# Bias rows from float32r parts over 128 rows, and vectors and filter turned in full blocks

## The chip, the cores and the metric

The kernel runs on one core of a Trainium2 chip. The metric is the device time of one execution in microseconds (us); 1726.06 us is the median of three runs of the kernel before. The core's engines are PE (TensorE, matrix products and transposes into PSUM), DVE (VectorE), ACT (ScalarE), POOL (GpSimd) and SP (which issues most transfers); each works through its own queue in order, and they wait for each other by semaphores. Transfers issued by POOL go through a queue of their own (q0 in the profile).

## The reference

One layer of a hybrid decoder trunk, with S = D = 1024, 8 heads and a convolution of width 31. Cut to what the change touches:

```python
h = rms_norm(x, attn_norm_w)
q, k, v, u, g = jnp.split(h @ w_in, splits, axis=-1)
...
rel = q_pos[:, None] - k_pos[None, :]
bias = jnp.transpose(bias_tab[t5_bucket(rel)], (2, 0, 1))      # bias_tab: rel_bias, 32 x 8
s = jnp.einsum('bhqd,bhkd->bhqk', qb, kf) * scale + bias
s = jnp.where(rel >= 0, s, -jnp.inf)                           # softmax, values, subln follow
...
c = causal_depthwise_conv(u_a * sigmoid(u_b), conv_w, conv_b)  # conv_w: 31 x 1024
c = silu(layer_norm(c, conv_ln_w, conv_ln_b))
y_b = c @ w_proj_conv
...
x = x + (sigmoid(g_a + b_a) * y_a + sigmoid(g_b + b_b) * y_b) @ w_out
x = x + (silu(gate) * up) @ w_down                             # gate, up from rms_norm(x)
```

The bias of a head depends on the distance of query and key alone, so it is one row of values for each head, laid out along the diagonals. Each bias row entry is `rel_bias` at the bucket of its distance, and a large negative number where the key lies ahead of the query. Inputs and outputs are float32.

## The kernel before

The program is one long stream of tiles of 128 partitions, written for each engine through a scheduler that sorts the instructions of each engine by a model of their times; `after(ins)` ties the instructions of a block behind an earlier one of their engine. Matrix products are made from float32r parts: an operand is split into a high part (ACT copies it to float32r, L120) and a low part (the difference, by DVE at L125 or by POOL at L131), and three products (high-high, high-low, low-high) are summed in PSUM (`mm3`, L167 to L170).

Order of the work around the change:

- `opening` (from L1084) loads and normalises the eight token tiles of x, turns them with full 128x128 transposes (`turn_x`, L724) and makes the first value columns (`v_tile`, L1110). After the third tile it calls `load_vectors` (from L229): POOL clears `rows` (64x128) and loads into it the small vectors, 128 numbers to a row (conv bias, layer-norm weight and bias, gate bias, subln, q and k norm), and into `cwrow` (31x1024) the convolution filter, a tap to a row. `vectors_last` is the last POOL instruction of that.
- At the end of `opening`, `vectors` (L256) turns them: one transpose of the 64 rows (L259), copied to `pvec`, where a vector is a column and so a scalar for each partition; and eight transposes of 31x128 (L267), copied to `cw`. Then the buffers of the opening are given back, and the pools `tt` and `st` are opened in their place.
- `first_stage` goes on with the remaining value columns (`v_item`, V1 and V2) and, for c = 1 to 7, `u_pair` (from L996): the convolution's input channels by a scheme of seven half-size products (L984) in place of eight. Their operands are sums and differences that POOL makes (L900 to L926 once, L965 to L968 for each pair) and splits (L131). A `u_pair` uses the half tiles `p1`, `u2` and `u3` of the pool `st`; `u2` has one buffer, the other two have two. ACT copies a product to `u2` at L1010 and to `u3` at L1013, and POOL multiplies them at L1021.
- Beside that, DVE runs the convolution, 31 taps a channel tile (`conv_taps`, L588 on ACT for the first, L594 on DVE for the others). The first four tiles are summed in PSUM, and ACT copies each to a tile `done` (L598), which has the single buffer of the tag `acc` in the pool `cv`; DMA stores it (L600).
- The loop over `first_stage` calls `bias_rows` at its steps 18, 19 and 20, each for 384 of the 1152 columns. `buckets` is an input of 33x1152 that holds one 1 in each column (the bucket of that distance, or row 32 where the key lies ahead). At the first call POOL fills `rb` (33x8) and loads `rel_bias` (L765, L766), and DVE changes its sign (L767). Each call then loads 384 columns of `buckets` into a half tile `u3` (L769), makes the product of `rb` and these in full float32, which runs as two matmul records (L771), copies the 8x384 result to a half tile `u2` (ACT, L772), and stores it to `b_d` (POOL, L773). Later `bias_skew` (L776) spreads each head's row over 128 rows of `t_d`, and `load_bias` reads it skewed, before the attention of that head.

The stages after that (attention beside the query, key and gate columns, the projections, the feed-forward part) are not touched.

Of the kernel before, what the change touches and what calls it, by code (L numbers as in the profile page):

```python
# [10 lines left out]
F32 = mybir.dt.float32  # L11
F32R = mybir.dt.float32r
AF = mybir.ActivationFunctionType
ALU = mybir.AluOpType
AX = mybir.AxisListType

P = 128
S = 1024
D = 1024
H = 8  # L20
HD = 64
VD = 128
CW = 31
FF = 2816
NFF = FF // P
NB = 32
EPS = 1e-6
LAM_INIT = 0.8 - 0.6 * math.exp(-0.3 * 0)
BIG = 1.0e30
# [28 lines left out]
def kernel(  # L58
# [57 lines left out]
    def f32(ap):  # L116
        return ap.bitcast(F32)

    def split_hi(dst, src):
        act.copy(dst, src)  # L120
# [3 lines left out]
    def split_lo(dst, src, hi):  # L124
        last_lo[0] = dve.tensor_tensor(dst, src, f32(hi), op=ALU.subtract).ins  # L125
# [9 lines left out]
    def after(ins):  # L135

        return nullcontext() if ins is None else tc.issue_after(ins)

    def last_of(engine):
        for ins in reversed(nc.cur_bb.bb.instructions):  # L140
            if ins.engine == engine:
                return ins
# [70 lines left out]
        act.copy(wb[:, 512 * g : 512 * (g + 1)], pt[:])  # L213

    NROW = 64
    rows = ap.tile([NROW, P], F32, name="rows", bufs=1)
    col = {}
    at = [0]

# [3 lines left out]
        col[key] = r0  # L223
        at[0] += n

    cwrow = ap.tile([CW, D], F32, name="cwrow", bufs=1)
    lamt = ap.tile([P, 4, HD], F32, name="lamt", bufs=1)

    def load_vectors():  # L229
        pool.memset(rows[:], 0.0)  # L230
        pool.dma_start(cwrow[:], conv_w[0])
        vec_rows("conv_b", conv_b, 8)
        vec_rows("ln_w", conv_ln_w, 8)
        vec_rows("ln_b", conv_ln_b, 8)
        vec_rows("gate_b", gate_b, 16)
        vec_rows("subln", subln_w, 1)
        for key, src in (("qn", q_norm_w), ("kn", k_norm_w)):
            r0 = at[0]
            for j in range(2):
                pool.dma_start(rows[r0 : r0 + 1, j * HD : (j + 1) * HD], src)  # L240
            col[key] = r0
            at[0] += 1
        for j, src in enumerate((lam_q1, lam_k1, lam_q2, lam_k2)):
            pool.dma_start(lamt[:, j, :], src.to_broadcast([P, HD]))
# [11 lines left out]
    def vectors():  # L256

        pt = pm()
        pe.transpose(pt[:, :NROW], rows[:], ident[:NROW, :NROW])  # L259
        dve.tensor_copy(pvec[:], pt[:, :NROW])  # L260
        dve.tensor_scalar(pcol("subln"), pcol("subln"), 1.0 - LAM_INIT, None, op0=ALU.mult)
        dve.tensor_scalar(pcol("kn"), pcol("kn"), -(HD ** -0.5), None, op0=ALU.mult)
        c_ = col["ln_w"]
        dve.tensor_scalar(pvec[:, c_ : c_ + 8], pvec[:, c_ : c_ + 8], -0.125, None, op0=ALU.mult)
        pt = pm()
        for k in range(NKT):
            pe.transpose(pt[:, k * 32 : k * 32 + CW], cwrow[:, k * P : (k + 1) * P], ident[:CW, :CW])  # L267
        dve.tensor_copy(
            cw[:, :, :CW], pt[:, : NKT * 32].rearrange("p (k t) -> p k t", t=32)[:, :, :CW]
        )  # L270
        for j in range(2):
            dve.tensor_tensor(lprod[:, j, :], lamt[:, 2 * j, :], lamt[:, 2 * j + 1, :], op=ALU.mult)
        dve.tensor_reduce(lsum[:], lprod[:], axis=AX.X, op=ALU.add)
# [461 lines left out]
    def tiles_from(pool_, names):  # L735
        return lambda: [pool_.tile([P, 512], F32R, tag=t_, name=nm(t_), bufs=2) for t_ in names]
# [14 lines left out]
    def v_item(j):  # L751
        halves = [ws.next(), ws.next()]
        for i2 in range(NT // 2):
# [3 lines left out]
            v_split(o, j, i2)  # L757
            yield

    rb = sm.tile([NB + 1, H], F32, tag="rb", name="rb", bufs=1)  # L760

    def bias_rows(c0):

        if c0 == 0:
            pool.memset(rb[:], -BIG)  # L765
            pool.dma_start(rb[:NB, :], rel_bias)  # L766
            dve.tensor_scalar(rb[:], rb[:], -1.0, None, op0=ALU.mult)  # L767
        oh, gr = half("u3")[: NB + 1, :384], half("u2")[:H, :384]
        pool.dma_start(oh, buckets[:, c0 : c0 + 384])  # L769
        o = pm()  # L770
        pe.matmul(o[:H, :384], rb[:], oh, start=True, stop=True)  # L771
        act.copy(gr, o[:H, :384])  # L772
        pool.dma_start(b_d[:, c0 : c0 + 384], gr)  # L773

    def bias_skew(h):
        pool.dma_start(t_d[h][:], b_d[h : h + 1, :].to_broadcast([P, TL]))  # L776
# [103 lines left out]
    def half(tag):  # L880
        return f32(st[0].tile([P, 512], F32R, tag=tag, name=nm(tag), bufs=1 if tag == "u2" else 2)[:])
# [202 lines left out]
    def opening():  # L1084
# [69 lines left out]
        )  # L1154
        with after(last_of(mybir.EngineType.Pool)):
            load_vectors()
        vectors_last = last_of(mybir.EngineType.Pool)
        xload(4)
        steps(
# [67 lines left out]
        tt.append(tt_ctx.enter_context(tc.tile_pool(name="tt", bufs=1, reuse_waits="tile")))  # L1227
        st.append(st_ctx.enter_context(tc.tile_pool(name="st", bufs=1, side="right", reuse_waits="tile")))
        v_tiles[0] = tiles_from(st[0], ("p1", "u3"))
        low_by_pool[0] = True  # L1230
        ws.ahead = 0
        yield from u_half(0, uw, 1)
# [5 lines left out]
    for _ in first_stage():  # L1238
        n += 1
        if n in (18, 19, 20):  # L1240
            with after(bias_anchor[0]):
                bias_rows(384 * (n - 18))
        if n >= 23 and n % 3 == 2 and (n - 23) // 3 < 2:
            with after(last_of(mybir.EngineType.Pool)):
                bias_skew((n - 23) // 3)
        due += 3.25
        with after(last_of(mybir.EngineType.DVE)):
            bg.step(int(due))
        due -= int(due)
# [889 lines left out]
```

## Time and profile before

| what | value |
|---|---|
| median of three runs | 1726.06 us (1725.62 to 1727.33) |
| the profiled execution's own time | 1724.98 us |
| its span in the trace | 1723.2 us |
| PE, share of the span busy | 99% |
| DVE, ACT, POOL | 74%, 51%, 13% |
| bias products (L771) | 6 records of 484 ns on average, 130.3 to 146.6 us |
| turn of the small vectors (L259, L267) | 9 transposes, 53.2 to 53.8 us |

The page gives, for each group of instructions, a line of the kernel, the engine, the operation, what is written from what, the shape of the operands (for matmuls also rows x columns of the weights), the count, and after the bar the time busy, the mean duration and the idle time ahead of it with what ended it. A timeline row has the start, the duration, the engine, line and operation, and in brackets the idle time before it and what released it. The half tiles appear there by the first letters of their tags (`u<-pm` is the copy of a bias row to `u2`).

### The profile page before, as it was taken

The page shows a single profiled execution, that of the slowest core. Times are in us where ns is not written, and L with a number is a line of the kernel's source. Part 1 is how long each engine was busy: PE and PEld are TensorE (multiplying, and loading weights), DVE is VectorE, ACT ScalarE, POOL GpSimd, SP SyncE. Part 2 cuts the span into 40 slices and gives each one's busy share as a digit, 9 for nine tenths or more (in the row PEclk, how much of TensorE's full clock was granted, in tenths as well). Part 3 has the DMA queues.
Part 4 walks back from the last instruction along what each step waited for, and adds up shares of the span by engine and source line. Part 5 has one row for each costly group of instructions (what it writes and reads, how often), then busy time and mean ns, then how long its engine had stood idle before and what let it go on. Part 6 is the DMA issues. An engine that isn't in the chain of part 4 may idle for free.

```text
span 1723.2 us, 25849 instructions
## 1 busy us (share of the span) xinstructions
PE 1713.9 (99%) x9243; PEld 1478.2 (86%) x9243; DVE 1276.2 (74%) x2128; ACT 873.2 (51%) x1958; POOL 219.2 (13%) x207
## 2 busy tenths in 40 slices
PE   9999999999999999999999999999999999999999
PEld 7997889998998998988788888888888888888887
DVE  7675889898988987977677769966666666575544
ACT  6333335767877886865556325633333333333332
POOL 4997851000000000000000000000000000000000
PEclk9999999999999999999999999999999999999999
DMA  6344445436345345354863683244455445597663
GB/s 209 117 128 134 131 151 143 113 103 174 107 128 147 116 125 148 99 146 145 316 225 128 196 301 108 77 141 156 149 174 167 153 143 165 175 371 271 216 217 128
DMA packets 261603, 281.64 MB, mean 163 GB/s; under 512 B 16545, under 2 KB 181985, under 8 KB 261474
## 3 DMA queue, kind: packets, MB, share of 16 engines
q1 hardware_dynamic: 254160, 267.71, 48.4%
q0 software_dynamic: 5680, 9.39, 2.6%
q10 hardware_dynamic: 1634, 2.89, 0.5%
q8 instruction: 73, 1.20, 0.3%
q14 instruction: 56, 0.46, 0.1%
HBM read 181.84 MB, written 85.50 MB: 155 GB/s over the span
## 4 chain that ended last, share of the span: by engine, by line
PE 93%; DVE 2%; DMA 2%; ACT 1%; issue 1%; SPq 0%; DVEq 0%; ACTq 0%
PE acc L984 30%; PE acc L488 12%; PE pg L168 12%; PE pg L170 12%; PE pg L169 12%; PE wo L1854 3%; PE sc L1294 2%; PE sc L1293 2%; PE pT L1332 2%; DVE acc L594 1%; PE pg L1110 1%; PE pW L168 1%; PE pW L170 1%; PE pW L169 1%; PE pQ L819 1%; DMA room<-in_w_out_dram 1%
## 5 line engine op out<-in xcount | busy, mean ns | idle before, releaser
L594 DVE SCALAR_TENSOR_TENSOR acc<-u,cw,acc 128x1023 f32<-128x1023 f32 (+14 forms) x240 | 303.5, 1264 | 23.0 <-ACT acc L588 20.4
L168 PE MATMUL pg<-whi,hT_hi 128*128 128x256 f32 x704 | 199.2, 284 | 0.8 <-DVE v L125 0.8
L169 PE MATMUL pg<-wlo,hT_hi 128*128 128x256 f32 x704 | 199.9, 284 | 0.0
L170 PE MATMUL pg<-whi,hT_lo 128*128 128x256 f32 x704 | 199.9, 284 | 0.0
L125 DVE TENSOR_TENSOR wlo<-draw,whi 128x1024 fp32r<-128x1024 f32 x75 | 91.8, 1224 | 86.0 <-ACT whi L120 78.6
L120 ACT CAST whi<-draw 128x1024 fp32r<-128x1024 f32 x75 | 79.1, 1055 | 129.5 <-PE acc L488 121.0
L168 PEld LDWEIGHTS pg<-whi,hT_hi 128*128 128x128 f32 x704 | 133.8, 191 | 2.6 <-DVE v L125 1.0
L169 PEld LDWEIGHTS pg<-wlo,hT_hi 128*128 128x128 f32 x704 | 134.2, 191 | 1.7
L170 PEld LDWEIGHTS pg<-whi,hT_lo 128*128 128x128 f32 x704 | 134.3, 191 | 1.5
L120 ACT CAST whi<-wraw 128x1024 fp32r<-128x1024 f32 x90 | 94.7, 1053 | 71.1 <-PE pg L169 37.0
L488 PE MATMUL acc<-wlo,whi 128*128 128x512 f32 x308 | 119.8, 389 | 0.0
L488 PE MATMUL acc<-whi,wlo 128*128 128x512 f32 x308 | 119.8, 389 | 0.0
L168 PE MATMUL pg<-hT_hi,whi 128*128 128x512 f32 x288 | 114.5, 398 | 0.0
L170 PE MATMUL pg<-hT_hi,wlo 128*128 128x512 f32 x288 | 113.9, 395 | 0.0
L169 PE MATMUL pg<-hT_lo,whi 128*128 128x512 f32 x288 | 113.9, 395 | 0.0
L1300 ACT ACTIVATE E<-E,mn 128x640 f32<-128x640 f32 (+7 forms) x128 | 99.5, 777 | 26.0 <-DVE mn L1295 25.6
L120 ACT CAST whi<-s 128x1024 fp32r<-128x1024 f32 x54 | 56.8, 1053 | 105.1 <-PE acc L984 102.0
L125 DVE TENSOR_TENSOR wlo<-wraw,whi 128x1024 fp32r<-128x1024 f32 x75 | 93.3, 1246 | 14.4 <-ACT whi L120 14.2
L984 PE MATMUL acc<-h_hi,whi 128*128 128x512 f32 x240 | 93.4, 389 | 0.0
L984 PE MATMUL acc<-h_lo,whi 128*128 128x512 f32 x240 | 93.4, 389 | 0.0
L1295 DVE CUSTOM_DVE_ANT_0 E<-sc,tb 128x512 f32<-128x512 f32 (+3 forms) x128 | 74.2, 585 | 23.6 <-PE pT L1332 13.8
L984 PE MATMUL acc<-h_hi,wlo 128*128 128x512 f32 x240 | 90.1, 389 | 0.0
(370 smaller groups left out, 4591.6 us busy)
## 6 DMA issues: line engine op xcount, KB each, us to landing
wraw<-in_w_gate_up_dram SPq DMA_DIRECT2D x44, 512.0 KB, 4.6
wraw<-in_w_in_dram SPq DMA_DIRECT2D x38, 512.0 KB, 4.1
qs<-qs SPq DMA_DIRECT2D x96, 128.0 KB, 2.3
wd<-in_w_down_dram SPq DMA_DIRECT2D x44, 256.0 KB, 3.1
tdT<-wd SPq DMA_DIRECT2D x88, 128.0 KB, 4.4
draw<-sdS SPq DMA_DIRECT2D x44, 256.0 KB, 3.8
draw<-tdT SPq DMA_DIRECT2D x44, 256.0 KB, 3.5
wraw<-in_w_in_dram SPq DMA_DIRECT2D x32, 256.0 KB, 3.2
```

The lines of the kernel that those rows point to most:

```text
L120: act.copy(dst, src)
L125: last_lo[0] = dve.tensor_tensor(dst, src, f32(hi), op=ALU.subtract).ins
L168: pe.matmul(o, lh, rh, start=start, stop=False)
L169: pe.matmul(o, lh, rl, start=False, stop=False)
L170: last_mm[0] = pe.matmul(o, ll, rh, start=False, stop=stop).ins
L488: m = pe.matmul(o[s_][i][:], l_[:, ts], r_[:, 512:], start=start and j + y_ == 0, stop=j == n - 1 and y_ == 2, skip_group_check=not start,)
L594: dve.scalar_tensor_tensor(a_, us[c][:, : S - n], cw[:, c, t : t + 1], a_, op0=ALU.mult, op1=ALU.add)
L984: last_mm[0] = pe.matmul(o[:], a_[x_][:, k, :], b_[y_][:, k, :], start=start and k + x_ + y_ == 0, stop=k == 3 and x_ == 1, skip_group_che ...
L1293: pe.matmul(o[:, :w], qh[:, qs], k, start=True, stop=False)
L1295: dve.tensor_tensor_reduce(e[:, ks], o[:, :w], tb[:, S - nk + c0 : S - nk + c0 + w], 1.0, mn[:, j : j + 1] if c0 else 3.0e38, ALU.add, ALU ...
L1300: act.activation(e[:, :nk], e[:, :nk], AF.Exp, bias=mn[:, j : j + 1], scale=-1.0, accum_out=l[:, j : j + 1])
L1854: last_mm[0] = pe.matmul(o[s_][i][:], A[u_], B[v_], start=start and j + y_ == 0, stop=j == 3 and y_ == 2, skip_group_check=not start,).ins
```

## The change

Three parts.

1. `rows` becomes 128x128, and its turn (L259) a full 128x128 transpose. `cwrow` becomes 128x2x128: the filter is loaded in four transfers, which put four blocks of 128 channels under each other, 32 partitions apart, and the eight transposes of 31 rows (L267) become two full ones. POOL clears `cwrow` first.
2. `bias_rows` makes each product as two float32r products, of a high and a low part of `rb` in 72 columns (8 of them used, the others zero), over all 128 rows (33 used, the others zero). The columns are cut as 512, 512 and 128 in place of three times 384. Only the first 8 rows of the result are copied.
3. The operands are made ahead: `bias_ones` loads the first 1024 columns of `buckets` into a cleared 128x1024 tile `oh`, right after `load_vectors`, in the buffer of the tag `acc`; `bias_tiles` clears and fills the two parts of `rb` and the last 128 columns of `buckets` (`tail`) when the pool `st` is opened. The load of `rel_bias` moves behind `load_vectors`, and `bias_rows` loads nothing.

```diff
-    rows = ap.tile([NROW, P], F32, name="rows", bufs=1)
+    rows = ap.tile([P, P], F32, name="rows", bufs=1)
...
-    cwrow = ap.tile([CW, D], F32, name="cwrow", bufs=1)
+    cwrow = ap.tile([P, 2, P], F32, name="cwrow", bufs=1)
...
         pool.memset(rows[:], 0.0)
-        pool.dma_start(cwrow[:], conv_w[0])
+        pool.memset(cwrow[:], 0.0)
+        for q in range(4):
+            pool.dma_start(
+                cwrow[32 * q : 32 * q + CW, :, :],
+                conv_w[0].rearrange("t (j q c) -> t q j c", q=4, c=P)[:, q],
+            )
...
-        pe.transpose(pt[:, :NROW], rows[:], ident[:NROW, :NROW])
+        pe.transpose(pt[:, :P], rows[:], ident[:])
...
-        for k in range(NKT):
-            pe.transpose(pt[:, k * 32 : k * 32 + CW], cwrow[:, k * P : (k + 1) * P], ident[:CW, :CW])
+        for j in range(2):
+            pe.transpose(pt[:, j * P : (j + 1) * P], cwrow[:, j, :], ident[:])
...
+    rb2 = []
+    MB = 72
+
+    def bias_ones():
+        oh = cv.tile([P, S], F32R, tag="acc", name="oh", bufs=1)
+        pool.memset(f32(oh[:]), 0.0)
+        pool.dma_start(oh[: NB + 1, :], buckets[:, :S])
+        rb2.append(oh)
+
+    def bias_tiles():
+        parts = st[0].tile([P, 2, MB], F32R, tag="rb2", name="rb2", bufs=1)
+        tail = st[0].tile([P, TL - S], F32R, tag="oht", name="oht", bufs=1)
+        for t_ in (parts, tail):
+            dve.memset(f32(t_[:]), 0.0)
+        pool.dma_start(tail[: NB + 1, :], buckets[:, S:])
+        with after(last_of(mybir.EngineType.DVE)):
+            dve.tensor_scalar(rb[:], rb[:], -1.0, None, op0=ALU.mult)
+        hi, lo = [parts[: NB + 1, z, :H] for z in range(2)]
+        split_hi(hi, rb[:])
+        split_lo(lo, rb[:], hi)
+        rb2.extend((parts, tail))
...
     def bias_rows(c0):
 
-        if c0 == 0:
-            pool.memset(rb[:], -BIG)
-            pool.dma_start(rb[:NB, :], rel_bias)
-            dve.tensor_scalar(rb[:], rb[:], -1.0, None, op0=ALU.mult)
-        oh, gr = half("u3")[: NB + 1, :384], half("u2")[:H, :384]
-        pool.dma_start(oh, buckets[:, c0 : c0 + 384])
+        cs, n = slice(c0, min(c0 + 512, TL)), min(512, TL - c0)
+        gr = half("u2")[:H, :n]
         o = pm()
-        pe.matmul(o[:H, :384], rb[:], oh, start=True, stop=True)
-        act.copy(gr, o[:H, :384])
-        pool.dma_start(b_d[:, c0 : c0 + 384], gr)
+        for z in range(2):
+            pe.matmul(o[:MB, :n], rb2[1][:, z, :], rb2[0][:, cs] if n == 512 else rb2[2][:], start=z == 0, stop=z == 1)
+        act.copy(gr, o[:H, :n])
+        pool.dma_start(b_d[:, cs], gr)
...
         with after(last_of(mybir.EngineType.Pool)):
             load_vectors()
+            pool.memset(rb[:], -BIG)
+            pool.dma_start(rb[:NB, :], rel_bias)
+            bias_ones()
         vectors_last = last_of(mybir.EngineType.Pool)
...
+        bias_tiles()
         low_by_pool[0] = True
...
-                bias_rows(384 * (n - 18))
+                bias_rows(512 * (n - 18))
```

## The prediction

> **What bounds the kernel now.** I read the head of the page first, then the busy times by stretch, then PE's timeline at the two places that the change touches, and last the other engines' rows beside them. The head of the page:
>
> ```profile
> span 1723.2 us, 25849 instructions
> ...
> PE 1713.9 (99%) x9243; PEld 1478.2 (86%) x9243; DVE 1276.2 (74%) x2128; ACT 873.2 (51%) x1958; POOL 219.2 (13%) x207
> ```
>
> PE (TensorE's matmuls) is busy 99% of the span; nothing else is near. Where PE's 9.3 us of idle time lie, the busy times by stretch tell, here for 60 to 1240 us (the columns: from:to, its length, then PE, PEld, DVE, ACT and POOL busy with their counts, granted clock, DMA share, GB/s):
>
> ```profile
> 60.00:150.00 90.00, 90.00 (x572) 79.92 (x571) 55.91 (x51) 34.70 (x45) 82.26 (x47) 1.00 0.44 140
> 150.00:300.00 150.00, 149.14 (x860) 131.93 (x859) 128.37 (x130) 64.93 (x138) 82.58 (x53) 1.00 0.47 137
> 300.00:820.00 520.00, 519.59 (x3472) 475.95 (x3471) 445.60 (x982) 377.88 (x1213) 19.45 (x73) 1.00 0.46 130
> 820.00:1000.00 180.00, 178.87 (x800) 146.74 (x799) 128.88 (x215) 91.36 (x146) 0.58 (x1) 1.00 0.63 209
> 1000.00:1240.00 240.00, 239.36 (x1087) 197.98 (x1086) 182.18 (x287) 104.07 (x165) 0.00 (x0) 1.00 0.48 160
> ```
>
> The stretch 60 to 150 us holds no idle time of PE at all, and both places of the change lie in or just before it. From 150 to 1240 us PE idles 0.86 + 0.41 + 1.13 + 0.64 = 3.04 us. The granted clock is 1.00 in each. So the price of an edit is the time that it adds to or takes from PE's queue, and every other edit counts only if it makes PE wait. A matmul's own duration misleads here, since matmuls overlap: what one costs is the distance between starts.
>
> **The turn of the small vectors.** PE's timeline around it:
>
> ```profile
> 51.16 1.12 PE L1110 MATMUL pg<-vwl,hT_hi 128*128 128x256 f32 x8
> 52.12 1.12 PE L1110 MATMUL pg<-vwh,hT_lo 128*128 128x256 f32 x8
> 53.17 0.27 PE L259 MATMUL pm<-ident,rows 64*128 64x64 f32 x1
> 53.37 0.67 PE L267 MATMUL pm<-ident,cwrow 31*128 31x31 f32 x8
> 53.97 0.50 PE L168 MATMUL pg<-hT_hi,whi 128*128 128x512 f32 x1
> 54.31 0.40 PE L169 MATMUL pg<-hT_lo,whi 128*128 128x512 f32 x1
> ```
>
> Eight 256-column products take 52.12 - 51.16 = 0.96 us, 0.12 each, so the place of the last ends at 53.08. L259 starts 0.09 later. It takes 0.20, the eight L267 take 0.60, and the first L168 after them holds PE for 0.34, where a 512-column product otherwise holds it 0.23 (below): 0.11 more. Together 1.00 us. After the change three full transposes stand there. Such a thing is in the trace:
>
> ```profile
> 41.27 1.04 PE L724 MATMUL px<-ident,xt 128*128 128x128 f32 x8
> 42.06 0.73 PE L1110 MATMUL pg<-vwl,hT_hi 128*128 128x256 f32 x4
> 42.62 1.11 PE L1110 MATMUL pg<-vwh,hT_lo 128*128 128x256 f32 x8
> ```
>
> Eight full transposes take 0.79 us (0.10 each), and the four products after them 0.56 where 4 x 0.12 = 0.48 would do: leaving the transposes costs 0.08. Three: 0.30 + 0.08 = 0.38 us. The term is 0.38 - 1.00 = **-0.62 us**.
>
> **The bias rows.** Three times, of which the first and the last are:
>
> ```profile
> 129.73 0.39 PE L984 MATMUL acc<-hT_lo,whi 128*128 128x512 f32 x1
> 129.96 0.39 PE L984 MATMUL acc<-hT_hi,wlo 128*128 128x512 f32 x1
> 130.28 0.81 PE L771 MATMUL pm<-u,rb 33*8 33x384 f32 x2
> 131.02 0.50 PE L984 MATMUL acc<-T4h,sh 128*128 128x512 f32 x1
> 131.35 0.39 PE L984 MATMUL acc<-T4l,sh 128*128 128x512 f32 x1
> ...
> 146.29 0.81 PE L771 MATMUL pm<-u,rb 33*8 33x384 f32 x2
> 147.03 0.50 PE L984 MATMUL acc<-hT_hi,wlo 128*128 128x512 f32 x1
> ```
>
> A 512-column product of two float32r operands holds PE for 129.96 - 129.73 = 0.23 us. One full-float32 product (two records, 33 rows) holds it for 0.74, the product before it for 0.32 (0.09 more) and the one after it for 0.33 (0.10 more): 0.93 us. The last one holds it for the same 0.74, so I count 3 x 0.93 = 2.79 us. Afterwards there are two pairs of 512 columns, 4 x 0.23 = 0.92, and one pair of 128 columns. That width in float32r stands in the attention stage:
>
> ```profile
> 372.43 0.22 PE L1293 MATMUL sc<-ks,qs 128*128 128x128 f32 x1
> 372.49 0.27 PE L1294 MATMUL sc<-ks,qs 128*128 128x128 f32 x1
> 372.60 0.45 PE L1293 MATMUL sc<-ks,qs 128*128 128x512 f32 x1
> ```
>
> They hold PE 0.06 and 0.11; a pair is 0.12 to 0.22, I take 0.17. No row shows weights of 128x72. Their bounds are nothing extra, as between any two full float32r products, and the 0.19 of the rows above for each of three groups (0.57). I take nothing, since both operands now fill all rows and have the neighbours' type. Sum 1.09, and the term is 1.09 - 2.79 = **-1.70 us** (-1.13 with the upper bound).
>
> The Trainium skill speaks against the filled rows: "TensorE: Matmul & The Clock Gate", section "Why this matters for your kernels", has a single matmul over 32 rows take the same time as one over 128, and "TensorEngine Tiling (Array Packing)", section "Key Properties", has a change of tiling mode drain the array. By the first, filling the rows gives nothing and the sum below would be that of rival 1; by the second, the 0.09 and 0.10 go and the sum stands. The trace bears out the second only in part: the full transposes, with no change of rows, also cost 0.08 on leaving.
>
> **What lies beside PE.** Rows of the timelines of POOL, DVE and ACT, those between them left out. First POOL ahead of its first sum:
>
> ```profile
> 13.12 0.72 POOL L231 DMA_DIRECT2D cwrow<-in_conv_w_dram  x1
> 15.98 0.13 POOL L765 MEMSET rb<- 33x8 f32 x1
> 22.95 0.51 POOL L766 DMA_DIRECT2D rb<-in_rel_bias_dram x1
> 36.78 0.19 POOL L1184 COPY seen<-xt 128x1 f32<-128x1 f32 x1 [13.32 <-DVE xt L714]
> ```
>
> The load of `rb` was issued at 22.95 already, so that move is nothing. New on POOL before 36.78 are three more issues of the filter (3 x 0.72 = 2.16), a 256-column and a 1024-column memset, and one bucket issue. A memset is bounded by 0.13 (8 columns) below and a whole sum over 1024 columns on POOL, 2.41 (below), above. Together 2.16 + 0.51 + two memsets are 2.9 to 7.5 us in 13.32 of idle time: nothing, and no loss either as long as it ends before 36.78. The filter's bytes stay the same, in shorter pieces, and are needed only at 53.4. Then DVE after the turn, and POOL at the last bias row:
>
> ```profile
> 60.61 1.99 DVE L125 TENSOR_TENSOR wlo<-wraw,whi 128x1024 fp32r<-128x1024 f32 x1 [1.37 <-ACT whi L120]
> 147.35 2.41 POOL L131 TENSOR_TENSOR wlo<-s,whi 128x1024 fp32r<-128x1024 f32 x1 [1.83 <-ACT whi L120]
> 149.72 0.54 POOL L773 DMA_DIRECT2D b_d<-u  x1
> ```
>
> DVE gets two memsets, the sign change (moved) and two small splits, ACT one small cast: each between POOL's 0.13 above and 0.28, the share of 144 columns in the 1.99 of 1024 (an estimate from that row), so about 1 us on DVE between 54 and 60 us. It idled 1.37 us ahead of 60.61: nothing, and at most that 1 us if the idle time were gone. POOL loses three bucket issues at 120 to 140 us and gets one for `tail`, which waits for a DVE memset with POOL's sums queued behind it, and for those ACT and PE; later POOL idles 1.83 us ahead of such a sum, so a stall there under that is hidden, and a longer one costs its excess.
>
> `oh` takes the one buffer of the tag `acc`, so ACT's copy L598 of the first convolution tile now waits for the second bias product:
>
> ```profile
> 125.15 1.02 ACT L598 COPY done<-acc 128x1024 f32<-128x1024 f32 x1 [0.46 <-DVE acc L594]
> 136.70 0.81 PE L771 MATMUL pm<-u,rb 33*8 33x384 f32 x2
> 140.41 1.21 ACT L588 ACTIVATE acc<-u,pvec,cw 128x1024 f32<-128x1024 f32 x1 [2.28 <-DMA u<-u_d]
> 151.49 0.59 ACT L1010 COPY u<-acc 128x512 f32<-128x512 f32 x1 [3.17 <-DMA b_d<-u]
> 154.88 0.39 PE L984 MATMUL acc<-T3h,whi 128*128 128x512 f32 x1
> ```
>
> The copy moves from 125.15 to about 137.4 and is done by 138.5, before L588, which waits for a transfer until 140.41: 1.9 us of cover, and nothing for PE.
>
> **Sum.** -0.62 - 1.70 = -2.32 us on PE. The profiled execution took 1724.98 us (span 1723.2 and 1.78 around it), the median of three runs is 1726.06; the sum moves either by the same. That execution would take 1722.66; it stands 1.08 under the median, so the forecast, made as a median, is 1726.06 - 2.32 = **1723.7 us**, 0.13% less. A measurement of this kernel can tell about 0.2%, 3.45 us, from no change.
>
> **The rivals.** (1) Filling the rows does not remove the 0.19 at each group: the bias term is -1.13, the sum -1.75, the time 1724.3. For it: the 0.08 after full transposes. Against it: the neighbours' type is the same now. The small-row rule of the Trainium skill's "TensorE: Matmul & The Clock Gate", told above, leads to this time.
>
> (2) The gain is given back in the chain through the single buffer `u2`: product, ACT's copy, POOL's store, landing, three times, and only then L1010, after which PE may go on in that bank at 154.88. For it: L1010 waited 3.17 us for the store, and the last store stands behind a sum of 2.41 us on POOL. The cover is 154.88 - 152.08 = 2.8 us, and PE now comes up to 1.7 us sooner: 1.1 is left. If the chain grows by 1.1 to 6.9 us, PE waits for up to 5.8 and the time lies between 1723.7 and 1729.5: I price it at 1726, below the middle, since three such delays are less likely than one. Against it: POOL is rid of three issues, and the third copy is of 128 columns.
>
> (3) The same chain, on the other side: if each of three stores falls behind one more such sum, 3 x 2.41 = 7.2 us, and the wait of 1.83 us for ACT comes with one of them, it grows by 9.0 us, PE loses 7.9, and the time is 1723.7 + 7.9 = **1731.6 us**. It is slower than before by over 0.2% from 6.9 us of growth.
>
> (4) Later waits close up: PE's 3.04 us of gaps from 150 to 1240 us come from other engines' order, which a new order may improve. All of them gone gives 1720.7; over 1.1 us of them is needed for 0.2%. For it: that order hangs on many waits. Against it: nothing in the change aims there, and gaps may grow as well.
>
> **How the numbers follow.** Forecast 0.47 (1722.9 to 1724.5), (1) 0.12, (2) 0.17, (3) 0.08, (4) 0.16. Faster by over 0.2% is (4), 0.16; slower is (3), 0.08; the rest, 0.76, is within. The range takes the forecast, (1), most of (2) and more than half of (4): 1721.4 to 1727.6.
>
> **What would show it.** The turn at 53 us should hold PE 0.4 us instead of 1.0, with no gap ahead of it. Each bias pair should hold it 0.46 (0.17 the narrow one), with neighbours at 0.23; a neighbour at 0.32 shows (1). PE's idle time between 60 and 150 us should stay at nothing, and L1010 should wait no longer than 3.2 us; PE idle after a bias row shows (2) or (3). The forecast is wrong if PE's idle time from 150 to 1240 us differs from 3.04 by more than 1 us.

## The result, and the profile after

The changed kernel takes 1740.77 us (median of five runs, 1740.29 to 1742.70) against 1726.06, a ratio of 1.0089 (95% interval 1.0078 to 1.0100): slower by 0.9%, where 1723.7 us had been forecast, a difference that a measurement can't tell from none. Four single executions on record, one each of the kernel before, turn_only, tail_sp and best2, took 3687 to 6091 us, and the ratios below leave them out. The head of the page after, with the PE row of the costliest groups that tells most:

```profile
span 1740.9 us, 25841 instructions
...
PE 1713.0 (98%) x9237; PEld 1479.3 (85%) x9237; DVE 1296.2 (74%) x2131; ACT 873.0 (50%) x1959; POOL 223.2 (13%) x211
...
L169 PE MATMUL pg<-wlo,hT_hi 128*128 128x256 f32 x704 | 201.0, 286 | 15.7 <-DVE wlo L125 15.7
```

PE is busy for as long as before (1713.0 against 1713.9 us), so the 17.7 us by which its span is longer are idle time: 1740.9 - 1713.0 = 27.9 us against 9.3. (The execution profiled is the slowest of the five, 1742.70 us; the medians differ by 14.7.) The last number of the L169 row says where: 15.7 us in a single wait, for DVE's split of a weight block (`wlo`, L125). The busy times by stretch, first the stretch that had no gap before, then the same cut at the gap (same columns as in the prediction):

```profile
60.00:150.00 90.00, 74.31 (x501) 69.54 (x500) 66.77 (x46) 27.22 (x35) 67.39 (x35) 0.91 0.33 103
```

```profile
66.30:82.20 15.90, 0.28 (x3) 0.07 (x1) 15.90 (x3) 0.30 (x1) 14.75 (x7) 0.60 0.00 1
82.20:86.50 4.30, 4.24 (x20) 4.24 (x21) 0.61 (x2) 0.00 (x0) 0.00 (x0) 0.50 0.56 183
86.50:100.00 13.50, 13.50 (x114) 13.50 (x114) 8.73 (x9) 6.10 (x7) 7.16 (x3) 1.00 0.49 157
```

From 66.3 to 82.2 us PE does nothing, and only DVE and POOL are "busy". Then, for 4.3 us, PE works at a granted clock of 0.50: twenty matmuls where a full clock does some 36 (0.12 us each). DVE's timeline there, and then POOL's:

```profile
59.99 2.06 DVE L781 TENSOR_SCALAR rb<-rb 33x8 f32<-33x8 f32 x1
62.36 18.72 DVE L125 TENSOR_TENSOR rb<-rb,rb 33x8 fp32r<-33x8 f32 x1 [0.31 <-ACT rb L120]
81.00 1.21 DVE L125 TENSOR_TENSOR wlo<-wraw,whi 128x1024 fp32r<-128x1024 f32 x1
```

```profile
61.98 0.54 POOL L779 DMA_DIRECT2D oht<-in_buckets_dram  x1
62.53 2.41 POOL L933 TENSOR_TENSOR F<-F,F 128x1024 f32<-128x1024 f32 x1
...
76.43 2.33 POOL L933 TENSOR_TENSOR F<-F,F 128x1024 f32<-128x1024 f32 x1
78.72 2.33 POOL L940 TENSOR_TENSOR T<-F,F 128x1024 f32<-128x1024 f32 x1
92.63 2.40 POOL L950 TENSOR_TENSOR T2l<-F,T2h 128x1024 fp32r<-128x1024 f32 x1 [11.58 <-ACT T2h L120]
```

The low part of the bias table, a difference of 33x8 numbers, is shown as 18.72 us of work. Most of such a row is a wait: a 128x1024 difference takes 1.21 us right behind it. It ends at 81.08, when POOL's last sum ends at 81.05 and POOL idles. It began while POOL was issuing the transfer of the `tail` (61.98 to 62.52), and eight sums without a pause lie between. So DVE's weight split stands behind a tiny difference, PE behind the weight split, and that difference behind POOL.

The two places of the change themselves did what the prediction said. PE at the turn, and around a wide and the narrow bias pair:

```profile
52.67 1.12 PE L1134 MATMUL pg<-vwh,hT_lo 128*128 128x256 f32 x8
53.63 0.27 PE L264 MATMUL pm<-ident,rows 128*128 128x128 f32 x1
53.74 0.38 PE L272 MATMUL pm<-ident,cwrow 128*128 128x128 f32 x2
53.88 0.48 PE L168 MATMUL pg<-hT_hi,whi 128*128 128x512 f32 x1
54.19 0.40 PE L169 MATMUL pg<-hT_lo,whi 128*128 128x512 f32 x1
...
153.49 0.40 PE L1008 MATMUL acc<-T1h,wlo 128*128 128x512 f32 x1
153.72 0.62 PE L795 MATMUL pm<-oh,rb 128*72 128x512 f32 x2
154.17 0.39 PE L1008 MATMUL acc<-hT_hi,whi 128*128 128x512 f32 x1
...
165.06 0.29 PE L795 MATMUL pm<-oht,rb 128*72 128x128 f32 x2
165.18 0.45 PE L1008 MATMUL acc<-T1h,whi 128*128 128x512 f32 x1
165.47 0.40 PE L1008 MATMUL acc<-T1l,whi 128*128 128x512 f32 x1
```

From the last L1134 group to L169 are 1.52 us, where 54.31 - 52.12 = 2.19 were: 0.67 less. A wide pair holds PE 0.45 us, the narrow one 0.12, with the neighbour ahead at 0.23 (the one behind the narrow pair at 0.29).

To see where the sum goes, each matmul of the trace after was paired with the same one of the trace before and the starts compared. A start in the trace after is later by +0.55 us at 52 us, -0.12 at 55 (the turn: -0.67), +17.67 at 72 (the stall: 17.8, of it 15.8 the gap and the rest slow clock), +16.03 at 200 (the bias rows: -1.64), and +16.57 or +16.58 from 1240 to the last matmul. The end of the span lies 1.1 us later still; that is the 17.7 us.

### The profile page after: what moved, and what is told of

It reads as the page before. It is cut to its first block, busy times and chain, and to the rows that moved or that the text cites. A ratio compares the mean times of both kernels' runs of the same rounds, so it can differ in the third digit from the quotient of the medians.

```text
span 1740.9 us, 25841 instructions
## 1 busy us (share of the span) xinstructions
PE 1713.0 (98%) x9237; PEld 1479.3 (85%) x9237; DVE 1296.2 (74%) x2131; ACT 873.0 (50%) x1959; POOL 223.2 (13%) x211
## 4 chain that ended last, share of the span: by engine, by line
PE 92%; DVE 2%; DMA 2%; issue 2%; ACT 1%; SPq 0%; DVEq 0%; ACTq 0%
PE acc L1008 30%; PE acc L493 12%; PE pg L168 12%; PE pg L169 12%; PE pg L170 12%; PE wo L1882 3%; PE sc L1322 2%; PE sc L1321 2%; PE pT L1360 2%; DVE acc L599 1%; PE pg L1134 1%; PE pW L169 1%; PE pW L170 1%; PE pW L168 1%; PE pQ L843 1%
## 5 line engine op out<-in xcount | busy, mean ns | idle before, releaser
L169 PE MATMUL pg<-wlo,hT_hi 128*128 128x256 f32 x704 | 201.0, 286 | 15.7 <-DVE wlo L125 15.7
L125 DVE TENSOR_TENSOR wlo<-draw,whi 128x1024 fp32r<-128x1024 f32 x75 | 91.8, 1223 | 86.0 <-ACT whi L120 80.7
L169 PEld LDWEIGHTS pg<-wlo,hT_hi 128*128 128x128 f32 x704 | 135.1, 192 | 17.6 <-DVE wlo L125 15.9
L169 PE MATMUL pg<-hT_lo,whi 128*128 128x512 f32 x288 | 113.8, 395 | 0.0
L125 DVE TENSOR_TENSOR wlo<-wraw,whi 128x1024 fp32r<-128x1024 f32 x75 | 92.8, 1240 | 13.0 <-ACT whi L120 12.7
```

The source lines that it names most:

```text
L169: pe.matmul(o, lh, rl, start=False, stop=False)
```

## The experiments

The theory that stood at the end: a DVE instruction that reads two SBUF operands and a POOL sum keep each other out; usually DVE gets in at the end of the running sum, but behind a transfer that POOL issued it doesn't, until POOL idles. (Two operands aren't needed to be kept out for a sum: the sign change L781 above reads one and took 2.06 us, until POOL's sum had ended at 62.02.) The rivals were that the form of the difference does it (its instruction, its 33 rows), the transfer's change of type or the landing of its bytes, or the difference itself wherever it stands. In the diffs below, names are those of the change.

**pool_lo: the same difference, made by POOL.**

```diff
-        split_lo(lo, rb[:], hi)
+        pool.tensor_tensor(lo, rb[:], f32(hi), op=ALU.subtract)
```

> The low part of rb (33x8) is made by POOL instead of DVE, at the same place; nothing else of any queue moves. Theory (lock-out): DVE's 18.72 us on this difference are waiting for POOL, which runs sums on SBUF operands back to back from 62.53 to 81.05 us; in POOL's own queue the difference takes under 0.5 us, DVE's next split runs at about 63 us, PE's gap of 15.69 us and the slow clock behind it (about 1.9 us) go, and the median is 1740.8 - 17.6 = 1723.2 us, 1722.5 to 1724.5. Rival (form): a difference over 33 rows and 8 columns is slow wherever it runs; then POOL is held for many us and the median stays above 1730.

Measured: 1741.26 us, ratio 1.0091 (1.0075 to 1.0108). POOL's difference took 0.22 us, but now the next DVE instruction was held:

```profile
62.37 0.54 POOL L779 DMA_DIRECT2D oht<-in_buckets_dram  x1
62.92 0.22 POOL L784 TENSOR_TENSOR rb<-rb,rb 33x8 fp32r<-33x8 f32 x1
```

```profile
63.71 18.99 DVE L125 TENSOR_TENSOR wlo<-wraw,whi 128x1024 fp32r<-128x1024 f32 x1 [1.26 <-ACT whi L120]
```

It isn't this instruction: the weight split, which also reads two SBUF operands, takes its place. The expectation of a cure was wrong.

**rows128: all 128 rows in place of 33.**

```diff
-        hi, lo = [parts[: NB + 1, z, :H] for z in range(2)]
+        hi, lo = [parts[:, z, :H] for z in range(2)]
...
-    rb = sm.tile([NB + 1, H], F32, tag="rb", name="rb", bufs=1)
+    rb = sm.tile([P, H], F32, tag="rb", name="rb", bufs=1)
```

> The sign change and the two splits of rb run over all 128 rows, still 8 columns, at the same place in the same queues. Lock-out: the rows don't matter; the difference on DVE still takes over 10 us and the run about 1740. Rival (form: 33 rows, an incomplete group of partitions): it takes at most one sum of POOL, as the products of lamt (128x64) did with 2.4 us each, and the run is about 1724.

Measured: 1742.34 us (one run), the difference held for 18.70 us. The number of rows doesn't matter.

**tail_late: the transfer at a later step.**

```diff
-        pool.dma_start(tail[: NB + 1, :], buckets[:, S:])
...
+        if n == 17:
+            with after(bias_anchor[0]):
+                pool.dma_start(rb2[2][: NB + 1, :], buckets[:, S:])
```

> POOL's transfer of the last 128 bucket columns, issued at 61.98 us just ahead of the sums, moves to the step before the first bias row (some 55 us later). Rival (transfer): the difference was passed over because POOL was issuing this transfer when it arrived; without it the difference waits for one sum at most (2.4 us), and the run is about 1724. Lock-out without regard to the transfer: the difference still takes over 10 us and the run stays about 1740.

Measured: 1740.32 us (one run), 18.72 us held. But the scheduler left the transfer at 62.27 us, so the run repeats the changed kernel and tells nothing.

**before_diff: the difference alone, in the kernel before.**

```diff
+        dm = sm.tile([NB + 1, 3, H], F32, tag="dm", name="dm", bufs=1)
+        with after(last_of(mybir.EngineType.DVE)):
+            dve.memset(dm[:], 1.0)
+        act.copy(dm[:, 1, :], dm[:, 0, :])
+        dve.tensor_tensor(dm[:, 2, :], dm[:, 0, :], dm[:, 1, :], op=ALU.subtract)
         low_by_pool[0] = True
```

> The kernel before, with nothing of the change, plus a memset, an ACT copy and one DVE difference over 33x8 numbers of a small tile at the place of the splits (outputs unused). Lock-out and form: this one small instruction is held for more than 7 us while POOL's sums run, PE gets a gap behind it, and the run is slower by several us, up to 17. Rival (transfer): there is no transfer by POOL here, so it is held for one sum at most (2.4 us) and the run is within 1 us of before.

Measured: 1730.48 us (one run; before 1725.08). The difference waits for one sum, and PE has no gap between 60 and 150 us:

```profile
63.38 1.77 DVE L1234 TENSOR_TENSOR dm<-dm 33x8 f32<-33x8 f32 x1 [0.48 <-ACT dm L1233]
```

So the difference alone doesn't bring the stall. The time is 5.4 us above, where within 1 us had been expected with a wait of one sum. By paired matmuls the 5 us have other places: 1.8 by 200 us, 1.0 more by 300, and 1.5 between 1240 and 1530, of which after_gap2 has more.

**tail_set: the changed kernel without the transfer.** The last 128 columns of `buckets` hold their 1 in row 32 alone, so DVE can set that row.

```diff
-        pool.dma_start(tail[: NB + 1, :], buckets[:, S:])
+        dve.memset(f32(tail[NB : NB + 1, :]), 1.0)
```

> The last 128 bucket columns hold a 1 in row 32 and nothing else, so a DVE memset of that row makes them, and POOL issues no transfer between its sums; POOL's queue is otherwise the same up to 90 us. (The run tail_late left the transfer at the same place, 62.27 us, so it could not tell.) Theory (transfer): only behind POOL's transfer do its sums keep DVE out at every boundary; without it DVE's split of rb waits for the end of one sum, at most 2.4 us, PE's gap of 15.69 us and the slow clock behind it go, and the median is about 17.6 us under the change, 0.1% under before (1723 to 1725 beside 1725 to 1726). Rival (back-to-back sums): the sums of this stretch keep DVE out whatever stands ahead of them; the gap stays and the median stays about 1740.

Measured: 1723.53 us (1722.26 to 1725.29, 11 runs), ratio 0.9994 (0.9985 to 1.0003). The stall is gone:

```profile
62.77 2.06 DVE L125 TENSOR_TENSOR rb<-rb,rb 33x8 fp32r<-33x8 f32 x1 [0.31 <-ACT rb L120]
64.76 1.21 DVE L125 TENSOR_TENSOR wlo<-wraw,whi 128x1024 fp32r<-128x1024 f32 x1
```

One instruction of POOL's, of 0.54 us, is worth 16.4 us here, each kernel taken beside its own runs of before. But this run alone doesn't tell the transfer from sums without a pause, since POOL also idled at the end of that sum, for ACT (the sum ahead ends at 64.81):

```profile
65.20 3.04 POOL L950 TENSOR_TENSOR T1l<-F,T1h 128x1024 fp32r<-128x1024 f32 x1 [0.39 <-ACT T1h L120]
```

The run tail_sp, below, has no such pause. What then keeps the kernel from a clear gain is, in PE's waits,

```profile
PE acc L1008 <- ACT u L796: 1.9, 2, 1.1
```

the chain through `u2` of rival (2), in small, and a start that comes 0.96 us later than before.

**both_set: tail_set with the 128x1024 clearing of `oh` at the program's start.**

```diff
-        oh = cv.tile([P, S], F32R, tag="acc", name="oh", bufs=1)
-        pool.memset(f32(oh[:]), 0.0)
+        oh = rb2.pop()
...
+        oh = cv.tile([P, S], F32R, tag="acc", name="oh", bufs=1)
+        pool.memset(f32(oh[:]), 0.0)
+        rb2.append(oh)
```

> As tail_set, and the clearing of oh (128x1024, 0.98 us on POOL at 15.80 us) moves to the start of the program, where POOL and DVE are idle. In the changed kernel DVE's small scaling L661 took 0.70 us in place of 0.17 and ended with that memset. Theory: this cost the start 0.54 us, and moved it is 0.4 to 0.6 us faster than tail_set. Rival: the start waits for something else then, and both take the same within 0.2 us.

Measured: 1723.43 us (11 runs), ratio 0.9990 (0.9981 to 0.9999). That is tail_set within the noise, where 0.4 to 0.6 us less had been expected. The root step L661 is back at 0.26 us (0.70 in the changed kernel, beside POOL's memset), but PE still reached the turn 1.0 us late, so the cause of the late start isn't settled. Its median is the lowest of all: 0.1% below the kernel before.

**turn_only: part 1 of the change alone.** The kernel before with `rows` of 128x128, `cwrow` of 128x2x128 in four transfers, and three full transposes.

> Part 1 alone: rows and filter turned in three full blocks, the bias rows as before. The term of the sum was -0.62 us on PE (1.00 us between the products around the turn becomes 0.38). Theory: no transfer by POOL stands between the sums, so nothing else follows, and the median is 0.3 to 1.0 us under before. Rival: three more transfer issues on POOL delay something at the start and the gain is given back, within 0.2 us of before or above it.

Measured: 1724.92 us, ratio 1.0000 (0.9991 to 1.0010). The turn takes the same 1.52 us as in the changed kernel; in the total the 0.67 us can't be told from nothing: the median is 0.27 us under that of before, between the 0.3 to 1.0 of the theory and the 0.2 of the rival.

**before_dma: the transfer alone, in the kernel before.**

```diff
+        dt = st[0].tile([P, P], F32R, tag="oht", name="oht", bufs=1)
+        dve.memset(f32(dt[:]), 0.0)
+        pool.dma_start(dt[: NB + 1, :], buckets[:, :P])
         low_by_pool[0] = True
```

> The kernel before, with nothing of the change, plus a tile of 128x128 that DVE clears and POOL fills with one transfer of 33x128 bucket columns at the place where the change has it (tile unused). Theory (transfer): behind this transfer POOL's sums keep out the next DVE instruction with two operands in SBUF (the split of a weight half near 61 us) until POOL has a gap, for more than 10 us, and the run is 10 to 18 us slower than before. Rival (back-to-back sums, or something else of the change): the split waits for one sum, and the run is within 5 us of before, as it was with a difference in place of the transfer.

Measured: 1725.03 us (one run), no stall. But the weight split was issued at 60.77 us, ahead of the transfer at 61.59, and no DVE instruction with two SBUF operands came behind it: it tests the price of the transfer (nothing), not the theory.

**before_both, then before_late: both pieces in the kernel before.** In before_both (the two diffs above together) the difference again ran ahead of the transfer (63.55 and 69.96 us).

> The kernel before with the two pieces together that it had singly in the runs before_dma and before_diff: DVE clears a 128x128 tile, POOL's transfer of 33x128 bucket columns into it stands among its sums, and behind that DVE makes a 33x8 difference of two SBUF tiles (its outputs are used by nobody). Theory (a DVE instruction with two SBUF operands that arrives behind a transfer issued by POOL is kept out of the following back-to-back sums until POOL idles): the difference is held for more than 10 us, PE gets a gap, and the time is 1732 to 1745 us. Rival (transfer and difference alone are harmless and so is the pair; something else of the changed kernel makes the stall): held for one sum at most, 2.4 us, and 1725 to 1730 us.

Measured: 1730.31 us (one run), held 1.77 us: it tells nothing beyond before_diff. In before_late the difference reads the landed bytes, so it must come behind:

```diff
+        pool.dma_start(dt[: NB + 1, :], buckets[:, :P])
+        act.copy(dm[:, 0, :], f32(dt[: NB + 1, :H]))
+        dve.tensor_tensor(dm[:, 1, :], f32(dt[: NB + 1, :H]), dm[:, 0, :], op=ALU.subtract)
```

> The kernel before with POOL's transfer among its sums as in before_both, and DVE's 33x8 difference now of the landed bytes and ACT's copy of them, so that it must come behind the transfer (its output is used by nobody). Theory (the transfer alone puts POOL's following sums ahead of any DVE instruction with two SBUF operands): the difference is held for more than 10 us, until POOL waits for something; the taps of the convolution behind it are late, and the time is 1730 to 1750 us. Rival (it needs something else of the changed kernel): held for one sum at most, 2.4 us, and 1725 to 1731 us.

Measured: 1742.17 us (one run). The difference was held for 7.52 us, until POOL idled. But another instruction had been held as well, and that one with no transfer in the 25 us ahead of it:

```profile
48.97 14.33 DVE L272 TENSOR_TENSOR lprod<-lamt 128x64 f32<-128x64 f32 x2
```

(4.78 us in the trace of before.) So the same kernel ran once more, for the spread:

> The kernel of before_late once more, for the spread of its times. If the two stalls there (DVE's L272 held 14.2 us with no transfer near it, and its difference held 7.5 us behind the transfer) come by chance: times in two or more groups, some runs at 1725 to 1731 us with neither stall and some at 1735 to 1745 us. If the order of this kernel brings them always: all runs at 1738 to 1745 us. If only the stall behind the transfer is regular: most runs at 1731 to 1740 us, and L272 at its usual 2.4 us in the profile.

Measured: 1742.75 us (1741.16 to 1743.50), ratio 1.0098 (1.0081 to 1.0115). L272 is at its usual 4.75 us here, and the difference is held for 17.11, POOL's sums running on from the transfer to 91.66:

```profile
74.57 17.11 DVE L1236 TENSOR_TENSOR dm<-oht,dm 33x8 f32<-33x8 f32 x1
```

```profile
69.75 0.56 POOL L1234 DMA_DIRECT2D oht<-in_buckets_dram  x1
...
89.31 2.35 POOL L131 TENSOR_TENSOR wlo<-wraw,whi 128x1024 fp32r<-128x1024 f32 x1
97.80 2.37 POOL L131 TENSOR_TENSOR wlo<-wraw,whi 128x1024 fp32r<-128x1024 f32 x1 [6.14 <-ACT whi L120]
```

The stall behind the transfer comes each time the two stand in that order, in the kernel before too. All runs lie in the 1738 to 1745 us that had been given for both stalls at once, and above the 1731 to 1740 of the one; it is L272's row in the profile that tells the cases apart, and the other runs have no profile. The difference here reads the bytes that landed, so the landing is over when the wait begins. L272's stall came in that one profile of the eighteen.

**tail_plain and tail_sp: a transfer without a change of type, and the same one issued by SP.** `plain` is a float32 tile, copied to `tail` by ACT; for room the bias parts have 32 columns.

```diff
-        pool.dma_start(tail[: NB + 1, :], buckets[:, S:])
+        pool.dma_start(plain[: NB + 1, :], buckets[:, S:])     # tail_plain
+        nc.sync.dma_start(plain[: NB + 1, :], buckets[:, S:])  # tail_sp
...
+        act.copy(tail[:], plain[:])
```

> The kernel after with the last 128 bucket columns loaded by POOL into a float32 tile, so that the transfer changes no type, and copied to float32r by ACT; to make room the bias parts have 32 columns in place of 72. Theory (any transfer that POOL issues there does it): the difference is held for some 18.7 us again and the time is 1738 to 1743 us. Rival (only a transfer that changes the type does it): held for one sum at most, 2.4 us, and 1723 to 1726 us.

> The kernel of tail_plain with the same 33x128 transfer issued by SP in place of POOL: the same bytes land in the same tile, and POOL's sums follow each other. Theory (POOL's issue ahead of its sums keeps DVE out): the difference is held for one sum at most, 2.4 us, no PE gap of 15 us, 1722 to 1726 us. Rival (the bytes that land in the middle of POOL's and DVE's work do it): held for more than 10 us, 1735 to 1743 us.

Measured: tail_plain 1741.39 us (one run), with the difference held 18.71 us; tail_sp 1724.73 us, ratio 0.9998 (0.9988 to 1.0007), held 2.05 us. DVE and POOL in tail_sp:

```profile
62.79 2.05 DVE L125 TENSOR_TENSOR rb<-rb,rb 33x8 fp32r<-33x8 f32 x1 [0.31 <-ACT rb L120]
64.77 1.21 DVE L125 TENSOR_TENSOR wlo<-wraw,whi 128x1024 fp32r<-128x1024 f32 x1
```

```profile
56.71 11.54 POOL L935 TENSOR_TENSOR F<-F,F 128x1024 f32<-128x1024 f32 x4
68.21 4.76 POOL L952 TENSOR_TENSOR T1l<-F,T1h 128x1024 fp32r<-128x1024 f32 x2
```

DVE got in amid POOL's sums, which follow each other without a pause here. The same bytes in the same tile do no harm if SP issues the transfer. It is POOL's issue, and not the type; that it isn't the landing, before_late shows. POOL's sums stand in another order here (four of L935 in a row); in after_gap2, below, they have the order of the changed kernel, and DVE got in as well.

**after_gap and after_gap2: a small POOL copy behind the transfer,** which waits for DVE's difference. after_gap copies into a new tile `gp` of the pool `sm`, after_gap2 into `rb`.

```diff
         split_lo(lo, rb[:], hi)
+        pool.tensor_copy(gp[:], f32(lo))
```

> The kernel after, its transfer kept, with one small POOL copy of the 33x8 low part right behind the transfer. It waits for DVE's difference, so POOL idles once between the transfer and the sums. Theory (POOL's idle time lets DVE in and ends the state): the difference takes under 1 us, the weight split behind it is held for one sum at most, PE has no gap of 15 us, and the time is 1723 to 1726 us. Rival (the transfer shuts DVE out for a time of its own, whatever POOL does behind it): the weight split is held for more than 10 us instead and the time stays at 1738 to 1743 us.

> The kernel of after_gap with POOL's small copy written into rb, which is not read any more, so that no tile is added to the pool sm. Both theories: no stall of DVE behind the transfer in most runs. If the extra tile (which moves the tiles behind it) made the 1.4 us between 1240 and 1530 us: they go, and the time is 1724.8 to 1725.8 us. If they belong to the pause: 1726.3 to 1727.2 us as before.

Measured: after_gap 1726.79 us, ratio 1.0019 (0.9998 to 1.0040), nine of ten runs at 1726.3 to 1727.9 (above the 1723 to 1726 expected) and one at 1746.24. after_gap2 falls in two groups: four runs at 1722.73 to 1723.75 and six at 1739.94 to 1744.16; its ratio of 1.0059 (1.0026 to 1.0092) is a mean over both. The granted clock tells the groups apart: 1.0 in the lower, 0.995 or 0.996 in the upper, as in every profile with the long stall (0.994 to 0.997). The profiled execution of after_gap2 is one of the lower group:

```profile
62.96 0.16 DVE L125 TENSOR_TENSOR rb<-rb,rb 33x8 fp32r<-33x8 f32 x1 [0.31 <-ACT rb L120]
63.92 2.90 DVE L125 TENSOR_TENSOR wlo<-wraw,whi 128x1024 fp32r<-128x1024 f32 x1 [0.80 <-ACT whi L120]
```

```profile
62.58 0.55 POOL L779 DMA_DIRECT2D oht<-in_buckets_dram  x1
63.19 0.18 POOL L785 COPY rb<-rb 33x8 f32<-33x8 f32 x1
63.34 2.40 POOL L934 TENSOR_TENSOR F<-F,F 128x1024 f32<-128x1024 f32 x1
65.71 3.38 POOL L951 TENSOR_TENSOR T1l<-F,T1h 128x1024 fp32r<-128x1024 f32 x1
```

DVE gets its difference done by 63.12, while POOL still issues the transfer (until 63.13). POOL's copy follows after 0.06 us, and DVE's weight split gets in at the next end of a sum; the POOL sum behind pays for it (3.38 in place of 2.40). So with the copy there the stall can stay away, but here only in four runs of ten, against the "most runs" expected. No profile shows a run of the upper group. The lower group also answers the side question: without the extra tile the 1.3 us that after_gap lost between 1240 and 1530 us are gone. (Its group is even lower than the 1724.8 to 1725.8 expected.) All five traces with a tile added to `sm` (after_gap, before_diff, before_both and the two of before_late) lose 1.3 to 1.6 there, so that loss goes with the tile; what moves by it and why it costs, no run shows.

**best2: tail_set with the copies of the bias rows in the two buffers `u3`.**

```diff
-        gr = half("u2")[:H, :n]
+        gr = half("u3")[:H, :n]
```

> The kernel of tail_set (the last row of the tail set by DVE, no transfer there) with the bias rows' copies in the two buffers u3 in place of the single u2. Theory (the 1.9 us that PE waited in tail_set for ACT to free the bank come from the chain copy, store, landing through the one buffer u2): these waits go, and the time is 1721.3 to 1722.8 us, 1 to 2 us under tail_set. Rival (the copies are late because of ACT's own queue, or the wait moves to the copies that use u3): no less than 1723 us.

Measured: 1726.41 us, ratio 1.0009 (1.0000 to 1.0018), 3 us above tail_set, with two runs at 1730.1. The waits for `u` are gone, and others take their place, the largest far from here:

```profile
PE pQ L843 <- DVE qkraw L835: 1.9, 1, 1.9
```

The 1.9 us were the chain's. That the order of later work ate the gain, as touchy as rival (4) had it but to the worse, is read from one profile.

## Why the prediction was wrong

- **The step that failed** is the one on DVE's small instructions: "about 1 us on DVE between 54 and 60 us ... nothing, and at most that 1 us if the idle time were gone". It added up durations and didn't ask what POOL would be running beside them. One of the "two small splits" reads two SBUF operands and stands behind a POOL transfer with POOL's sums queued after it; it took 18.72 us, and PE lost 17.8. The transfer had been priced as an issue of 0.5 us with a wait for a memset, "hidden" under POOL's later idle time; its effect on DVE was in no rival. Without it (tail_set) the time is 1723.53 us, 1.7 below its own runs of before.
- **Signs of it were in the trace of before.** The 128x1024 split takes 1.99 us beside POOL's sums, where the one behind the stall takes 1.21, and two 128x64 products take 4.78 (the row below). Each of them shows a wait for one sum; nothing in that trace shows a wait for eight. The 1.99 was used as a duration ("the share of 144 columns in the 1.99"), and not read as a wait.

```profile
48.75 4.78 DVE L272 TENSOR_TENSOR lprod<-lamt 128x64 f32<-128x64 f32 x2
```

- **What it had named as its signs.** PE's idle time from 60 to 150 us, which "should stay at nothing", became 15.7 us. The one sign said to refute the forecast, PE's idle time from 150 to 1240 us, stayed within its 1 us (0.06 + 1.42 + 1.47 + 0.60 = 3.55 in place of 3.04): it looked behind the stall.
- **The turn** was right: -0.67 us, predicted -0.62, in the changed kernel and in turn_only.
- **The bias rows** were right: -1.64 by the paired matmuls, predicted -1.70. The wide pairs cost 0.45 (0.46), the narrow one 0.12 (0.17). The 0.19 at the wide groups is gone, and the narrow one keeps 0.06 behind it, so rival (1) did not come about. Rows and type of the operands changed together, and no run parts them: which of the two removed it, and so which of the two rules of the Trainium skill named there holds, stays open.
- **"Nothing" for POOL's additions at the start** was wrong too: PE comes 0.55 to 1.55 us later to the turn in the eleven traces of the changed kernel and its variants, and 0.09 to 0.46 later in the six of the kernel before with other additions. In turn_only, with part 1 alone, it is 0.09, so the filter's three issues aren't it. In the changed kernel DVE's root step L661 took 0.70 beside POOL's memset of `oh` in place of 0.17; with that gone (both_set) PE came 1.0 late all the same.
- **The rivals** (2) and (3) looked at POOL's sums, but at what they do to the stores of the bias rows, well behind the stall, and not at what they do to DVE. Rival (2) appears as 1.9 us in tail_set, where it had been priced at up to 5.8. The copy L598 and `acc` made no wait of PE, as predicted.
- **Where the stall stays away, the total comes out near the sum, in part by luck.** The lower group of after_gap2 is at 1722.73 to 1723.75 us, about 2 below its 1725.3 of before, and 2.32 was the sum. By paired matmuls of its profile, the turn gives -0.67 and the bias rows -1.58, near their terms; the start loses 1.13, and work from 200 to 1240 us gains 1.08, neither of which was forecast, and they cancel.

## What to carry to other kernels

Before adding a DVE instruction whose operands all lie in SBUF, look at what POOL runs at that moment, and before adding a transfer to POOL's queue amid a run of sums, look at which DVE instructions come behind it; give the transfer to SP, or make the bytes some other way. A row whose duration is many times that of larger ones of its kind is mostly a wait: read which engine's row ends at the same time. A cheap instruction's price is that of the queue that stands behind it.

## What the chip showed

- **DVE kept out by POOL, sum after sum.** A wait for one sum is ordinary (33x8 differences of 1.77 to 2.06 us); 18.7 us, the length of eight sums, was not expected. "SBUF — State Buffer" of the Trainium skill, section "SBUF: two separate sides", calls the port pair that the two share an exclusive lock, which a GpSimd instruction, a DVE instruction in a mode that uses both ports, or one with two SBUF inputs (against a GpSimd instruction that reads SBUF, as these sums do) holds for its whole length. The waits for one sum agree with that, and so do the DVE instructions with an operand in PSUM, which took 0.68 us beside the same sums. The rule says nothing of a waiter that is passed over at seven ends in a row, as here.
- **POOL's issue makes it near certain, and isn't the whole cause.** With POOL's transfer ahead of the held instruction and its sums right behind, all 17 runs (5 of the changed kernel, 4 of pool_lo, one each of rows128, tail_late and tail_plain, 5 of before_late) took 1739 to 1744 us, and the seven profiles among them show the stall; of the changed kernels without that transfer on POOL (tail_set, both_set, tail_sp, best2) none took as long. But L272 was passed over five times with no transfer near it. Why a transfer favours it stays open; another short POOL instruction in its place was tried only in after_gap and after_gap2, behind the transfer and with a pause.
- **The clock after the gap.** Behind 15.7 us without work PE ran at a granted clock of 0.50 for 4.3 us, and lost some 2 us more. "TensorE: Matmul & The Clock Gate", section "What's actually happening", has the gate fall to half after an idle window of about 3.4 us and rise after as long of busy time. The trace agrees roughly: PE's last matmul before the gap starts at 66.30, the granted clock is 1.00 until 69.4 and 0.50 from 69.5, and it stays 0.50 for 4.3 us of work, from 82.2 to 86.5 us.
